# Attention steps of a hybrid diffusion layer: a finished tile's bank counts as free one step later, and two readouts are queued behind the maximum of their own step

## The chip, the core and the metric

The program runs on one core of a Trainium2 chip. The time is the device time of one execution in microseconds (us). The kernel before took 1681.66 us, the median of three runs (1681.48, 1681.66, 1682.79).

## What is computed

Two layers of a backbone work on 512 latent tokens with a prefix of 256 context tokens. The change lies in layer 0, whose mixer has two groups of heads that share one input projection and one output projection: four heads of gated linear attention (GLA, two pairs) and eight heads of softmax attention.

```python
def _gated_readout(o, og, gain):
    return _merge(_rms(o, gain) * jax.nn.silu(og))

def _softmax_attend(q, k, v):
    s = jnp.einsum('bhgqd,bhkd->bhgqk', q, k, preferred_element_type=jnp.float32) * (ATT_HEAD_DIM ** -0.5)
    p = jax.nn.softmax(s, axis=-1).astype(v.dtype)
    return jnp.einsum('bhgqk,bhkd->bhgqd', p, v)

    a_lat = _gated_readout(dirs[0][1] + dirs[1][1], og[:, :, n_ctx:], gla_out_norm)
    ...
    o_lat = jnp.concatenate([a_lat, b_lat], axis=-1)
```

A latent query sees all 768 keys, a context query the 256 context keys. The readout of the GLA heads is a root mean square over the 128 columns of a head, times a gate; its gain comes in later.

## The kernel before

**Order of the work.** `even_mixer` writes TensorE's order by hand: generators, one letter each, are advanced by `run("...")`, and every matmul and transpose that they issue is kept in that order. What VectorE (DVE), ScalarE (ACT), GpSimd (POOL) and the DMA queues do is traced in the same order, but a scheduler decides where each instruction then stands in its engine's queue; it may put an instruction forward to where its inputs are expected ready. A queue is worked off in its order. `issue_after(ins)` keeps the instructions of a block behind `ins` on the engine of `ins`; on other engines it does nothing. `net.mark` is the latest such `ins` that some helper left.

**A step of the attention over latent tokens** (`Attention.latent`, letter "y"). There are four tiles of 128 queries (t = 0 to 3) and eight heads, so step i, from 0 to 36, has head i % 8 of tile i // 8:

- `scores` multiplies the head's queries with all keys into a tile S (two buffers of two PSUM banks each), DVE takes the maximum of each row (`amx`, line 193; the keys carry a minus sign, so it is written as a minimum), ACT takes the exponential and its sum (line 195), DVE inverts the sum (`ars`, line 196) and scales the row (`prob`, line 198).
- `turned` transposes the probabilities of the head three steps earlier (j = i - 3) on TensorE: four blocks of 128 keys into a bank with the tag "tr", then two blocks into one of two banks "sc0" and "sc1". ACT copies each part out to `probT` (line 210); for every fourth head (j % 4 = 3) DVE copies the second part.
- `values`, in every other step, multiplies the probabilities of two heads with the values. It adds into the tile `attO`, which for query tile t is the whole bank "sc" t % 2 for eight steps.
- After a tile's fourth pair (step 11, 19, 27, 35) `done` reads that bank twice: ACT writes the rounded half (line 734), and DVE subtracts it from the bank for the rest (line 735).

`other()` picks the bank for the two last blocks of `turned`. As long as tile t is not in `ended` it is the bank that tile t does not use; once t is in `ended`, it is tile t's own bank, since the next tile is about to take the other one. `done` enters the tile in `ended`, so the next step's transposes (step 12, 20, 28) already go to the bank that `done` is reading. The first `values` of tile t + 1 come in step 13, 21, 29.

The 256 context queries come first, in wider steps (`Attention.context`, letter "x"), through the same helpers.

**The readouts.** `readout(c, (t0,))` treats two tiles of tokens of the pair of heads c: ACT squares (line 1188), DVE sums (`ss`, line 1190), DVE scales and adds (`ms`, line 666), POOL raises to the power -1/2 (`rs`, line 668), DVE multiplies (`gvo<-gvo,rs`, line 1193) and multiplies with the gate (`gvo<-gvo,og`, line 1195). For the second pair, c = 1, the letter is "r1"; its three parts (context tokens, latent tiles 0 and 1, latent tiles 2 and 3) are advanced behind steps 7, 10 and 15:

```python
            behind = {6: "t", 7: "r1", 9: "t", 10: "r1", 14: "M", 15: "r1", 16: "M", 17: "t", 19: "t", 22: "t", 24: "t", 26: "t", 29: "t"}
            for i in range(3, 32 + 5):
                run("y " + behind.get(i, ""))
```

The transposes "t" (`catT`, lines 1290 and 1291) read what the readouts write: the second pair's from step 22 on. "M" is a product for the modulation of the next part (`mod_acc`), which in step 14 has 64 matmuls.

Of the kernel before, what the change touches and what calls it, by code (L numbers as in the profile page):

```python
# [13 lines left out]
ALU = mybir.AluOpType  # L14
AX = mybir.AxisListType
# [118 lines left out]
class Attention:  # L134
# [43 lines left out]
    def scores(self, t, heads, p):  # L178

        nc, net = self.nc, self.net  # L180
        s = net.mm_tile("S")
        nk = p.shape[-1]
        w = 1024 // len(heads)
        for x, hd in enumerate(heads):
            at = w * x
            for ks in self.k[int(t >= LT)]:
                m = ks[0].shape[-1]
                for i, k in enumerate(ks):
                    net.mm(s[:, at : at + m], self.q[t][:, hd, :], k[:, hd // 4, :], start=(i == 0), stop=(i == 1))
                at += m  # L190
        sv = s.rearrange("p (x k) -> p x k", k=w)[:, :, :nk]
        mx, sm, r = (net.sm.tile([P, len(heads)], F32, tag=tag, name=tag) for tag in (("amx", "asm", "ars") if len(heads) == 1 else ("ms4", "ss4", "rs4")))
        nc.vector.tensor_reduce(mx, sv, axis=AX.X, op=ALU.min)
        for x in range(len(heads)):
            nc.scalar.activation(p[:, x, :], sv[:, x, :], AF.Exp, bias=mx[:, x : x + 1], scale=-1.0, accum_out=sm[:, x : x + 1])
        nc.vector.reciprocal(r, sm)
        for x in range(len(heads)):
            nc.vector.tensor_scalar(p[:, x, :], p[:, x, :], r[:, x : x + 1], None, op0=ALU.mult)
# [30 lines left out]
                )  # L229

    def done(self, t):
        self.ended.append(t)
        self.net.put(self.cat, slice(4, 8), slice(t * P, (t + 1) * P), self.po[t].rearrange("p (j i) -> p j i", j=4))

    def context(self):
# [38 lines left out]
        values(1)  # L274
        yield
        self.done(LT)
        turned(2)
        yield
        values(2)
# [1 line left out]
        yield  # L281
        values(3)
        self.done(LT + 1)

    def latent(self, ap):
        kl = [ap.tile([P, 2, SEQ], F32R, name=f"k{x}") for x in "HL"]
# [5 lines left out]
        yield  # L292

        ahead = 3
        ps, pTs, due = {}, {}, []
        for i in range(8 * LT + ahead + 2):
            t, hd = divmod(i, 8)
            if t < LT:
                ps[i] = ap.tile([P, NT], F32, tag="prob", bufs=4, name="prob")
                self.scores(t, (hd,), ps[i][:, None, :])  # L300
            j = i - ahead
            if 0 <= j < 8 * LT:
                pTs[j] = ap.tile([P, NTT, P], F32, tag="probT", bufs=4, name="probT")
                self.turned(ps.pop(j), pTs[j], (1,) if j % 4 == 3 else (), self.other())
            if due:
                t0, n, xs = due.pop()
                self.values(t0, n, xs)
                if n == 3:
                    self.done(t0)
            if 0 <= j < 8 * LT and j % 2:  # L310
                due.append((j // 8, j // 2 % 4, [pTs.pop(x) for x in (j - 1, j)]))
            if t + 1 < LT and hd == 4:
                self.queries(t + 1, q(t + 1))
            yield


class Net:
# [761 lines left out]
    def even_mixer(self, h, mix, z):  # L1079
# [102 lines left out]
        def readout(c, tiles=tiles):  # L1182
# [12 lines left out]
                nc.vector.scalar_tensor_tensor(x, x, 0.5 if c else 1.0, og[c][:, t0 : t0 + 2, :], op0=ALU.mult, op1=ALU.mult)  # L1195


        kinds = {
            "q": lambda: nat(1536 + 288, ev_q), "kv": lambda: nat(1536 + 544, ev_kv), "m": lambda: mods,
            "qk0": lambda: qk(0), "qk1": lambda: qk(1), "v0": lambda: values(0), "v1": lambda: values(1),  # L1200
            "g0": lambda: gates(0), "g1": lambda: gates(1), "p": lambda: self.att_prep(mixg, natq, natk),
            "c0": lambda: job(0, 0), "l0": lambda: job(0, 1), "c1": lambda: job(1, 0), "l1": lambda: job(1, 1),
            "e": decays, "r0": lambda: (readout(0, (t,)) for t in tiles), "r1": lambda: (readout(1, (t,)) for t in tiles),
            "x": lambda: att.context(), "y": lambda: att.latent(ap),
            "t": lambda: self.gated_T(lambda t, hh: gv[:, t, hh * P : (hh + 1) * P], 4, R_GG, cat, ((4, 2), (0, 4))),
            "M": lambda: self.mod_group(0, 4, ["wL"] * 4 + ["wH"] * 3 + ["raw"]),
# [999 lines left out]
```

## Time and profile before

| | |
|---|---|
| median of the runs | 1681.66 us |
| time of the profiled execution | 1680.08 us |
| its span in the trace | 1678.3 us |
| mean granted TensorE clock | 0.999 |
| TensorE busy | 1638.8 us, 98% of the span |
| DVE, ACT, POOL busy | 1312.2 us, 916.9 us, 122.6 us |
| attention over latent tokens | from about 256 us to 348 us of the span |

A row of the timeline has the start in us from the span's start, the time it took, engine, line, operation, output and inputs, their size and the number of instructions; in brackets stands the time that the engine was idle just before, and who ended it. Rows of one engine overlap a little, since an engine begins an instruction before the last one has fully ended. So what an instruction costs its queue is the distance to the next start, which is less than the duration by some 0.08 us on DVE and ACT.

### The profile page before, as it was taken

The page shows a single profiled execution, that of the slowest core. Times are in us where ns is not written, and L with a number is a line of the kernel's source. Part 1 is how long each engine was busy: PE and PEld are TensorE (multiplying, and loading weights), DVE is VectorE, ACT ScalarE, POOL GpSimd, SP SyncE. Part 2 cuts the span into 40 slices and gives each one's busy share as a digit, 9 for nine tenths or more (in the row PEclk, how much of TensorE's full clock was granted, in tenths as well). Part 3 has the DMA queues.
Part 4 walks back from the last instruction along what each step waited for, and adds up shares of the span by engine and source line. Part 5 has one row for each costly group of instructions (what it writes and reads, how often), then busy time and mean ns, then how long its engine had stood idle before and what let it go on. Part 6 is the DMA issues. An engine that isn't in the chain of part 4 may idle for free.

```text
span 1678.3 us, 32400 instructions
## 1 busy us (share of the span) xinstructions
PE 1638.8 (98%) x13347; PEld 1474.3 (88%) x13347; DVE 1312.2 (78%) x2104; ACT 916.9 (55%) x1560; POOL 122.6 (7%) x129
## 2 busy tenths in 40 slices
PE   6999998999999999999999999999999999999998
PEld 5889987888999999998887788888888899999886
DVE  4889768966898989778668648788775499987887
ACT  4745557846544443445447536566564565555564
POOL 1004210001000000002101000000000100000310
PEclk9999999999999999999999999999999999999999
DMA  9651002154253446249516542111115334433973
GB/s 331 193 155 41 2 28 101 52 198 152 90 151 101 134 148 193 78 136 222 101 56 210 193 132 64 52 54 50 52 56 159 117 113 122 115 101 101 223 166 138
DMA packets 184736, 204.77 MB, mean 122 GB/s; under 512 B 7143, under 2 KB 141837, under 8 KB 184589
## 3 DMA queue, kind: packets, MB, share of 16 engines
q1 hardware_dynamic: 173632, 181.82, 34.6%
q0 software_dynamic: 9024, 17.30, 5.9%
q10 hardware_dynamic: 1932, 3.59, 0.6%
q8 instruction: 104, 1.70, 0.4%
q14 instruction: 44, 0.35, 0.1%
HBM read 193.23 MB, written 9.46 MB: 121 GB/s over the span
## 4 chain that ended last, share of the span: by engine, by line
PE 84%; DVE 7%; ACT 4%; DMA 2%; issue 2%; POOL 1%; DVEq 0%; ACTq 0%; POOLq 0%
PE nat L355 12%; PE a L355 11%; PE ff L355 8%; PE E L355 8%; PE x L355 6%; PE oproj L355 6%; PE o L355 4%; PE b L355 4%; PE D L355 4%; PE pearly L355 3%; PE fq L355 3%; PE gqk L355 2%; PE q L355 2%; PE S L355 2%; PE poh L355 1%
## 5 line engine op out<-in xcount | busy, mean ns | idle before, releaser
L355 PE MATMUL nat<-wH,x 128*128 128x256 f32 (+2 forms) x968 | 226.1, 322 | 3.1 <-ACT x L734 2.6
L355 PEld LDWEIGHTS nat<-wH,x 128*128 128x128 f32 x968 | 162.0, 190 | 20.5 <-ACT x L734 4.2
L824 ACT CAST wH<-raw 128x1024 fp32r<-128x1024 f32 x120 | 124.9, 1051 | 99.0 <-DVE raw L849 37.6
L825 DVE TENSOR_TENSOR wL<-raw,wH 128x1024 fp32r<-128x1024 f32 x120 | 145.7, 1221 | 23.2 <-ACT wH L824 22.6
L355 PE MATMUL nat<-wL,x 128*128 128x256 f32 (+2 forms) x484 | 153.5, 317 | 1.8 <-DVE wL L770 1.8
L770 DVE TENSOR_TENSOR wL<-raw,wH 128x1024 fp32r<-128x1024 f32 (+1 forms) x83 | 98.7, 1198 | 49.7 <-ACT wH L769 49.0
L355 PE MATMUL ff<-x,wH 128*128 128x512 f32 (+1 forms) x512 | 127.7, 340 | 0.0
L769 ACT CAST wH<-raw 128x1024 fp32r<-128x1024 f32 (+1 forms) x83 | 84.9, 1035 | 70.6 <-PE ff L355 19.9
L668 POOL TENSOR_TENSOR rs<-ms,neghalf 128x1 f32<-128x1 f32 (+2 forms) x62 | 64.7, 1049 | 791.1 <-DVE ms L666 791.0
L355 PE MATMUL oproj<-wH,x 128*128 128x512 f32 x320 | 102.3, 396 | 0.6 <-ACT x L1290 0.6
L355 PEld LDWEIGHTS nat<-wL,x 128*128 128x128 f32 x484 | 92.1, 190 | 7.9 <-DVE wL L770 2.7
L355 PEld LDWEIGHTS ff<-x,wH 128*128 128x128 f32 x512 | 87.2, 190 | 10.0
L597 DVE SCALAR_TENSOR_TENSOR macc<-mraw,scT,macc 128x1024 f32<-128x1024 f32 x70 | 88.0, 1280 | 8.8 <-DMA mraw<-in_mod_w_dram 8.4
L355 PE MATMUL x<-wH,two 128*128 128x512 f32 x280 | 90.6, 392 | 0.8 <-DVE y L1801 0.7
L976 ACT COPY qkh<-arr 128x512 f32<-128x512 f32 x112 | 70.1, 642 | 36.4 <-DVE arr L981 32.2
L1723 POOL DMA_DIRECT2D t<-in_ffn_w_down_dram x36 | 41.8, 1198 | 637.2 <-DVE t L1762 337.5
L355 PE MATMUL ff<-x,wL 128*128 128x256 f32 (+1 forms) x256 | 86.2, 337 | 0.0
L849 DVE TENSOR_TENSOR raw<-raw 128x512 f32<-128x512 f32 x120 | 82.8, 690 | 2.8
L981 DVE TENSOR_TENSOR arr<-arr,f 128x512 f32<-128x512 f32 x112 | 74.2, 687 | 1.9 <-ACT qkh L976 0.3
L355 PEld LDWEIGHTS oproj<-wH,x 128*128 128x128 f32 x320 | 59.5, 188 | 12.8 <-ACT x L1290 1.1
L355 PE MATMUL E<-x,wH 128*128 128x384 f32 (+1 forms) x320 | 70.7, 310 | 0.0
L355 PE MATMUL b<-x,wH 128*128 128x384 f32 (+1 forms) x320 | 70.6, 310 | 0.0
(420 smaller groups left out, 4530.2 us busy)
## 6 DMA issues: line engine op xcount, KB each, us to landing
mraw<-in_mod_w_dram SPq DMA_DIRECT2D x80, 512.0 KB, 4.1
raw<-in_ffn_w_gate_dram SPq DMA_DIRECT2D x44, 512.0 KB, 4.8
raw<-in_ffn_w_up_dram SPq DMA_DIRECT2D x44, 512.0 KB, 4.4
raw<-in_odd_w_in_dram SPq DMA_DIRECT2D x40, 512.0 KB, 3.7
t<-in_ffn_w_down_dram POOLq DMA_DIRECT2D x30, 512.0 KB, 8.7
raw<-in_ffn_w_down_dram SPq DMA_DIRECT2D x28, 512.0 KB, 7.9
mraw<-in_mod_w_dram SPq DMA_DIRECT2D x32, 256.0 KB, 6.3
raw<-in_even_w_in_dram SPq DMA_DIRECT2D x16, 512.0 KB, 6.8
```

The costliest lines, as they stand in the source:

```text
L355: return self.pin(self.nc.tensor.matmul(*a, **k))
L597: nc.vector.scalar_tensor_tensor(a, u, w, a, op0=ALU.mult, op1=ALU.add)
L668: nc.gpsimd.tensor_tensor(rs, ms, self.neghalf.to_broadcast([P, w]), op=ALU.pow)
L769: nc.scalar.copy(H[:, :m], raw[:, :m])
L770: nc.vector.tensor_tensor(L[:, :m], raw[:, :m], H[:, :m].bitcast(F32), op=ALU.subtract)
L824: self.nc.scalar.copy(H, f)
L825: self.nc.vector.tensor_tensor(L, f, H.bitcast(F32), op=ALU.subtract)
L849: add = lambda o, x, y: nc.vector.tensor_tensor(o, x, y, op=ALU.add)
L976: nc.scalar.copy(qkv[:, :, :, half, :], dst)
L981: nc.vector.tensor_tensor(dst, dst, tb, op=ALU.mult)
L1723: add = lambda o, src: self.pin(nc.gpsimd.dma_start(out=o, in_=src, accum_op=ALU.add))
```

## The change

Two things. First, `done` no longer enters its tile in `ended`. In `latent` it is entered one step later, after that step's transposes have picked their bank; in `context` it is entered right behind `done`, as it was. Second, the parts of "r1" are traced with their DVE instructions kept behind the maximum (`amx`) of the step in which they are advanced, for which `scores` leaves that instruction in `net.mark`.

```diff
-        nc.vector.tensor_reduce(mx, sv, axis=AX.X, op=ALU.min)
+        net.mark = nc.vector.tensor_reduce(mx, sv, axis=AX.X, op=ALU.min)
...
     def done(self, t):
-        self.ended.append(t)
         self.net.put(self.cat, slice(4, 8), slice(t * P, (t + 1) * P), self.po[t].rearrange("p (j i) -> p j i", j=4))
...
         self.done(LT)
+        self.ended.append(LT)
...
         self.done(LT + 1)
+        self.ended.append(LT + 1)
...
-        ps, pTs, due = {}, {}, []
+        ps, pTs, due, past = {}, {}, [], []
...
+            now = []
             if due:
                 t0, n, xs = due.pop()
                 self.values(t0, n, xs)
                 if n == 3:
                     self.done(t0)
+                    now.append(t0)
+            self.ended += past
+            past = now
...
+        def later():
+            for t in tiles:
+                with self.tc.issue_after(self.mark.ins):
+                    readout(1, (t,))
+                yield
...
-            "e": decays, "r0": lambda: (readout(0, (t,)) for t in tiles), "r1": lambda: (readout(1, (t,)) for t in tiles),
+            "e": decays, "r0": lambda: (readout(0, (t,)) for t in tiles), "r1": later,
```

The change adds eleven lines, so the same statement has a higher line number after it: 735 becomes 740, 1190 becomes 1195, 1193 becomes 1198, 1195 becomes 1200; lines up to 231 keep theirs.

On DVE, at the passage from the context queries to the latent ones, two of the three readouts stood before like this (`kL` and `qs` are keys and queries for the latent steps, `x_3656` is `done` of the first context tile, `probT_3659` the copy of transposed probabilities of the context's third block):

```order
L210 COPY probT_3551<-pT 128x512 [waits PE_49]
L1190 TENSOR_REDUCE ss_3922<-sq 128x4
L1190 TENSOR_REDUCE ss_4023<-sq 128x4 [waits Activation_49]
L666 TENSOR_SCALAR ms<-ss_3922 128x4 [waits DVE_49]
...
L162 SCALAR_TENSOR_TENSOR kL<-kT,kH 64x512 [waits Activation_49]
L175 TENSOR_TENSOR qs_3592<-qT,qs_3592 64x512 [waits Activation_49]
L1193 TENSOR_TENSOR gvo<-gvo,rs 128x2x256 [waits Pool_49]
L1195 SCALAR_TENSOR_TENSOR gvo<-gvo,og_656 128x2x256 [waits DVE_49]
L735 TENSOR_TENSOR x_3656<-attO,x_3655 128x4x128 [waits PE_49,Activation_49]
L1178 SCALAR_TENSOR_TENSOR og_656<-og_656,nat 128x512 [waits Activation_49]
L210 COPY probT_3659<-pT 128x512 [waits PE_49]
```

After the change the same place on DVE has no readout:

```order
L210 COPY probT_3551<-pT 128x512 [waits PE_49]
L196 RECIPROCAL rs_3540<-ss_3539 128x4 [waits Activation_49]
...
L162 SCALAR_TENSOR_TENSOR kL<-kT,kH 64x512 [waits Activation_49]
L175 TENSOR_TENSOR qs_3592<-qT,qs_3592 64x512 [waits Activation_49]
L740 TENSOR_TENSOR x_3656<-attO,x_3655 128x4x128 [waits PE_49,Activation_49]
L1183 SCALAR_TENSOR_TENSOR og_656<-og_656,nat 128x512 [waits Activation_49]
L210 COPY probT_3659<-pT 128x512 [waits PE_49]
```

Four instructions of each of the two readouts have left this place, and so have their two on POOL; the squares on ACT have not moved. The third readout, behind step 15, stands between the same DVE instructions as before.

The second of the two moved readouts (`ss_4023`) now stands on DVE in steps 10 to 12, from the DVE copy of step 10 to `done` of query tile 0 (`x_3656`), which had only `amx`, `ars` and `prob` ahead of it:

```order
L210 COPY probT<-pT 128x256 [waits PE_49]
L1195 TENSOR_REDUCE ss_4023<-sq 128x4
L193 TENSOR_REDUCE amx<-S 128x1 [waits PE_49]
L196 RECIPROCAL ars<-asm 128x1 [waits Activation_49]
L671 TENSOR_SCALAR ms<-ss_4023 128x4 [waits DVE_49]
L198 TENSOR_SCALAR prob<-prob,ars 128x768 [waits DVE_49]
L1198 TENSOR_TENSOR gvo<-gvo,rs 128x2x256 [waits Pool_49]
L196 RECIPROCAL ars<-asm 128x1 [waits Activation_49]
L193 TENSOR_REDUCE amx<-S 128x1 [waits PE_49]
L1200 SCALAR_TENSOR_TENSOR gvo<-gvo,og_656 128x2x256 [waits DVE_49]
L198 TENSOR_SCALAR prob<-prob,ars 128x768 [waits DVE_49]
L740 TENSOR_TENSOR x_3656<-attO,x_3655 128x4x128 [waits Activation_49]
```

The first one (`ss_3922`) stands in the same manner among the `amx`, `ars` and `prob` of steps 7 to 9, ahead of that copy. On TensorE the order of these steps is the same; what the two last blocks of steps 12 and 13 wait for is not. Before, from the scores of step 12 on (`qs_3808` are the queries of tile 1):

```order
L358 MATMUL pT<-ident,prob 128x128 x4
L358 MATMUL pT<-ident,prob 128x128 [waits DVE_49,PE_49]
L358 MATMUL pT<-ident,prob 128x128
L358 MATMUL qT<-ident,natq 128x128 [waits Activation_49]
L358 MATMUL qT<-ident,natq 128x128 x3
L355 MATMUL S<-kH,qs_3808 128x512 [waits Activation_49]
...
L358 MATMUL pT<-ident,prob 128x128 [waits Activation_49]
L358 MATMUL pT<-ident,prob 128x128 x3
L358 MATMUL pT<-ident,prob 128x128 [waits Activation_49]
```

And after:

```order
L363 MATMUL pT<-ident,prob 128x128 x4
L363 MATMUL pT<-ident,prob 128x128 [waits Activation_49]
L363 MATMUL pT<-ident,prob 128x128
L363 MATMUL qT<-ident,natq 128x128 x4
L360 MATMUL S<-kH,qs_3808 128x512 [waits Activation_49]
...
L363 MATMUL pT<-ident,prob 128x128 [waits DVE_49,Activation_49]
L363 MATMUL pT<-ident,prob 128x128 x3
L363 MATMUL pT<-ident,prob 128x128 [waits DVE_49]
```

The wait of the fifth block for DVE has passed from step 12 to step 13, and step 12 waits for an ACT copy. Steps 20 and 28 change in the same way. At the end of the stage three matmuls of the output projection, which stood together between the two parts of step 32's transposes, are now spread: one between the parts of step 31's, one in step 32, one in step 33.

## The prediction, on record before the run

> **What bounds the kernel.** I begin with the page: the busy time of the engines, and the shares of the chain that ended last.
>
> ```profile
> PE 1638.8 (98%) x13347; PEld 1474.3 (88%) x13347; DVE 1312.2 (78%) x2104; ACT 916.9 (55%) x1560; POOL 122.6 (7%) x129
> ...
> PE 84%; DVE 7%; ACT 4%; DMA 2%; issue 2%; POOL 1%; DVEq 0%; ACTq 0%; POOLq 0%
> ```
>
> TensorE (PE) is busy for 98% of the span, and the chain runs on it for 84%. A change that touches no matmul can gain only what PE waits. So the next view is the table of windows over the stage that changes (window, its length, then busy time and instructions of PE, weight loads, DVE, ACT, POOL).
>
> ```profile
> 250.00:262.00 12.00, 9.93 (x89) 8.64 (x89) 10.87 (x19) 4.31 (x8) 2.96 (x5) 1.00 0.44 139
> 270.00:280.00 10.00, 9.76 (x102) 8.25 (x97) 8.89 (x17) 8.33 (x19) 0.00 (x0) 1.00 0.01 2
> 280.00:290.00 10.00, 8.42 (x77) 7.14 (x72) 7.73 (x15) 7.55 (x17) 0.00 (x0) 1.00 0.00 0
> ```
>
> From 250 to 262 us, where two readouts stand, DVE is nearly full and PE idles for about 2 us. From 270 to 290, where the change puts them, DVE works 16.6 of 20 us: room, but not much. The waits of PE from 235 to 352 us (total, times, longest) name the idle time:
>
> ```profile
> PE pT L358 <- DVE x L735: 2.1, 3, 1.3
> PE attO L355 <- DVE probT L210: 1.4, 1, 1.4
> PE pT L358 <- DVE kL L162: 0.6, 1, 0.6
> ```
>
> All three are waits for DVE, and the change touches each.
>
> **Part one: two readouts leave the passage.** DVE and PE there, from the timeline:
>
> ```profile
> 246.98 1.27 DVE L1190 TENSOR_REDUCE ss<-sq 128x4 f32<-128x512 f32 x2
> 248.17 0.29 DVE L666 TENSOR_SCALAR ms<-ss 128x4 f32<-128x4 f32 x2
> 249.51 0.69 DVE L1193 TENSOR_TENSOR gvo<-gvo,rs 128x512 f32<-128x512 f32 x1 [0.87 <-POOL rs L668]
> 252.95 1.14 DVE L1195 SCALAR_TENSOR_TENSOR gvo<-gvo,og 128x512 f32<-128x512 f32 x1
> 254.12 0.69 DVE L162 SCALAR_TENSOR_TENSOR kL<-kT,kH 64x512 fp32r<-64x512 f32 x1
> 255.57 0.69 DVE L1193 TENSOR_TENSOR gvo<-gvo,rs 128x512 f32<-128x512 f32 x1
> 256.30 0.69 DVE L1195 SCALAR_TENSOR_TENSOR gvo<-gvo,og 128x512 f32<-128x512 f32 x1
> 257.02 0.69 DVE L735 TENSOR_TENSOR x<-attO,x 128x512 fp32r<-128x512 f32 x1
> 258.22 0.68 DVE L210 COPY probT<-pT 128x512 f32<-128x512 f32 x1
> ...
> 254.96 1.35 PE L358 MATMUL pT<-ident,prob 128*128 128x128 f32 x8 [0.61 <-DVE kL L162]
> ...
> 258.96 0.66 PE L355 MATMUL attO<-probT,natk 128*64 128x128 f32 x8 [1.36 <-DVE probT L210]
> ```
>
> PE waits 0.61 us for the second `kL`, which ended at 254.81. Ahead of it went the wait for POOL with a multiplication (0.87 us idle, then 0.69 us) and the 1.14 us gate. Without them it ends more than 2 us earlier; PE's own matmuls fill its time until 254.35, so all of the 0.61 goes.
>
> The second wait, 1.36 us, is for the copy at 258.22. The two `gvo` rows at 255.57 and 256.30 hold DVE for 257.02 - 255.57 = 1.45 us directly ahead of the three instructions that end in this copy. Without them, and behind a `kL` that is no longer late, the copy ends at about 256.9, when PE, itself 0.61 us earlier, wants it (258.96 - 1.36 - 0.61 = 257.0). I leave 0.1 us of wait. **Term one: -0.61 - 1.36 + 0.10 = -1.87 us.** With the bounds 0 (DVE finds something else to be late with) and -1.97 this is the term I trust most, since nothing else moves on DVE there. The readouts issue no DMA. Their squares stay in two buffers until `ss` has read them; the next to want one is the third readout's square in step 15, when both are free.
>
> **Part two: the first readout in steps 7 to 9.** It adds to DVE's queue `ss` (two starts 0.60 us apart, since 1.27 us for two that overlap by 0.08), `ms` (0.12) and the two `gvo` rows (0.72 each, from the starts 255.57, 256.30, 257.02): 2.16 us. What DVE had free between step 7 and the copy of step 10, at 283.11, shows in the brackets:
>
> ```profile
> 276.30 0.16 DVE L196 RECIPROCAL ars<-asm 128x1 f32<-128x1 f32 x1 [0.39 <-ACT prob L195]
> 276.79 0.96 DVE L193 TENSOR_REDUCE amx<-S 128x1 f32<-128x768 f32 x1 [0.33 <-PE S L355]
> 280.44 0.16 DVE L196 RECIPROCAL ars<-asm 128x1 f32<-128x1 f32 x1 [0.55 <-ACT prob L195]
> 281.58 0.75 DVE L1291 SCALAR_TENSOR_TENSOR x<-catT,col,x 128x512 fp32r<-128x512 f32 x1 [0.32 <-ACT x L1290]
> ```
>
> 0.39 + 0.33 + 0.55 + 0.32 = 1.59 us, and `ss`, put between an `ars` and the scaling that waits for it, fills another 0.12. What is late is then the copy of step 10, by 2.16 - 1.59 - 0.12 = 0.45 us, for which PE already waits 0.27 (the row at 283.58 below). Bounds: 0, if steps 8 and 9 have slack that no bracket shows, and 2.16, if none of the free time can be used. **Term two: +0.45.**
>
> **Part three: the bank and the second readout.** Steps 10 to 13 in the timeline:
>
> ```profile
> 283.11 0.41 DVE L210 COPY probT<-pT 128x256 f32<-128x256 f32 x1
> 283.44 0.95 DVE L193 TENSOR_REDUCE amx<-S 128x1 f32<-128x768 f32 x1
> 283.58 0.44 PE L358 MATMUL pT<-ident,prob 128*128 128x128 f32 x2 [0.27 <-DVE probT L210]
> ...
> 285.54 0.38 ACT L210 COPY probT<-pT 128x256 f32<-128x256 f32 x1
> 285.88 0.62 DVE L198 TENSOR_SCALAR prob<-prob,ars 128x768 f32<-128x768 f32 x1
> 286.22 0.60 PE L358 MATMUL pT<-ident,prob 128*128 128x128 f32 x4
> 287.29 0.68 DVE L735 TENSOR_TENSOR x<-attO,x 128x512 fp32r<-128x512 f32 x1
> 288.12 0.41 PE L358 MATMUL pT<-ident,prob 128*128 128x128 f32 x2 [1.30 <-DVE x L735]
> 288.37 0.60 PE L358 MATMUL qT<-ident,natq 128*128 128x128 f32 x4
> 288.72 0.48 PE L355 MATMUL S<-kH,qs 128*128 128x512 f32 x1
> 289.51 0.82 PE L358 MATMUL pT<-ident,prob 128*128 128x128 f32 x6
> ```
>
> Step 12 wants the bank that `done` reads, and waits 1.30 us for the subtraction at 287.29. In the other bank its last reader is the ACT copy that ends at 285.92, before PE's 286.8: this wait goes. The wait that takes its place is in step 13, whose last blocks need the finished bank. PE would be there at 286.8 + 0.25 (two transposes, 288.12 to 288.37) + 0.35 (`qT`) + 0.79 (`S`) + 0.43 (four blocks) = 288.6 us. With DVE's old order the bank is free at 287.97 and step 13 finds it so.
>
> But the second readout now stands ahead of the subtraction. From the copy's start at 283.11: 0.33 to the next start, `ss` 0.60, `amx` 0.87, `ars` 0.08, which puts `ms` at 284.99. From `ms` to the multiplication there is a round through POOL; before, it took from 248.17 to 249.51, 1.34 us, and only one scaling fills it. Then `gvo` 0.72, `ars` 0.07, `amx` 0.87, `gvo` 0.72, `prob` 0.54 (285.88 to 286.42), the subtraction 0.68: 284.99 + 1.34 + 3.60 = 289.9, and PE restarts some 0.15 later, as it did at 288.12 after 287.97. That is 290.1 against 288.6: a new wait of about 1.5 us in place of 1.30. Bounds: 0, if POOL answers in the time of the scaling and DVE starts without a backlog; 2.8, if the 0.6 us round through POOL falls in twice and nothing overlaps. I take the sum. **Term three: -1.30 + 1.50 = +0.20.** The 64 matmuls of step 14 then cover DVE's backlog; without that cover it would go on into steps 15 and 16.
>
> Steps 20 and 28 have no readout. Step 20 never waited (the 2.1 us above are three waits, and the first, 0.29 us, is for a context tile, whose order in `ended` stays). Step 28 waited here:
>
> ```profile
> 331.51 0.44 PE L358 MATMUL pT<-ident,prob 128*128 128x128 f32 x2 [0.49 <-DVE x L735]
> ```
>
> Step 29 is some 1.4 us behind it and the subtraction is over by then. **Term four: -0.49**, with 0 as its other end if the matmul of the output projection that now stands in step 31 waits for its weights instead.
>
> **The sum** against the profiled execution is -1.87 + 0.45 + 0.20 - 0.49 = -1.71, so 1680.08 - 1.71 = 1678.4 us. The median of the runs is 1.58 us above that execution; the same change gives **1680.0 us**, 0.10% faster. What measurements of this kernel can tell from no change is about 0.2%, 3.4 us.
>
> **The rivals.**
>
> *All waits go.* DVE fits both readouts in, and terms two and three become 0 and -1.30: -1.97 - 1.30 - 0.49 = -3.76, 1677.9 us. For it speaks that DVE had 3.4 free us from 270 to 290; against it, that the second readout stands directly ahead of the subtraction. 0.25.
>
> *DVE becomes the bound of steps 7 to 13* and the kernel is slower. Its rows there wait for ACT's exponentials, so perhaps none of the free time is free at the right moment. Then the readouts cost 2.16 us and 2.16 + 0.6 us (POOL) in full, 4.92, against -1.87 - 1.30 - 0.49: +1.26, 1682.9 us. The point from which it decides: the waits removed come to 3.66 us, so the change loses once less than 1.26 us of DVE's free time can be used. 0.11.
>
> *The change does not do what it says in the total.* What attention wins is lost at the next place that cannot come earlier, a load above all: 1681.7 us. Over the whole run PE's list of waits has one DMA, at the start:
>
> ```profile
> PE pt_rows L358 <- DMA rows<-in_mod_b_dram: 8.0, 1, 8.0
> ```
>
> This speaks against it. 0.08.
>
> *DVE and POOL block each other.* Two rows show what the scaling `prob` does beside POOL. The first is its group from the tile's view (minimum, median, maximum in ns); the second ran inside POOL's round of the third readout, which is the row behind it.
>
> ```profile
> L198 DVE TENSOR_SCALAR prob<-prob,rs x16: 342/348/700, 230.0 to 251.3; 128x256 f32<-128x256 f32 x16
> ...
> 301.84 0.61 DVE L198 TENSOR_SCALAR prob<-prob,ars 128x768 f32<-128x768 f32 x1
> ...
> 301.21 1.28 POOL L668 TENSOR_TENSOR rs<-ms,neghalf 128x4 f32<-128x4 f32 x1 [45.72 <-DVE ms L666]
> ```
>
> One of the 16 took 0.70 us instead of 0.35; the one beside `rs` took its usual 0.61. If the scalings in the new places were held until `rs` is done, the multiplications would start 0.54 us after POOL instead of at once, less what they lose anyway: 0.36 in the first readout and 0.51 in the second, together +0.87, 1680.9 us. [...] 0.08.
>
> **How the numbers follow.** My forecast has 0.48. The range 1677.6 to 1682.6 reaches from just below the case in which all waits go to just short of the one in which DVE is the bound, and takes in the bounds of terms two and three one at a time. Faster by over 0.2% (below 1678.3) is most of the first rival, 0.18, and 0.03 of the forecast with a larger term: 0.21. Slower by over 0.2% (above 1685.0) needs the DVE rival with more than its price: 0.05. Within 0.2%: 0.74.
>
> **What would show it.** In the profile after, the waits of 0.61 and 1.36 us at the passage are gone and PE runs through from 249 to 262 us (term one). The wait for `probT` in step 11 is about 0.7 us (term two). PE's wait for the subtraction, now line 740, is no longer in step 12 but in step 13, at some 1.5 us (term three), and it is gone in step 28 (term four). I am wrong if step 13 does not wait, if new waits for `amx` or for ACT's exponentials appear between 272 and 300 us, or if the output projection begins 1.7 us earlier and the end does not.

## The result and the profile after

The changed kernel took 1679.54 us, the median of 20 runs (1678.13 to 1680.67), against 1681.74 us for the kernel before, the median of 20 runs (1680.07 to 1683.45). The ratio is 0.9987 with a 95% interval of 0.9981 to 0.9993: 2.20 us, 0.13%, faster. The forecast was 1680.0 us, 0.10%.

The two profiled executions do not show that: 1680.08 us before, 1680.65 us after. The first lies 1.66 us below the median of its kernel, the second 1.11 us above the median of its own. A part of that stands outside the stage that changed: the first row below starts 0.72 us later after the change, and another 1.1 us go between 1370 and 1412 us of the span. So the stage has to be read by itself, from one matmul ahead of the passage to one at its end. Three rows of TensorE's timeline serve for it: the transposes `kT` ahead of the passage, the 64 matmuls of step 14, and the last matmuls of `attO`. Before the change (the fourth row is step 13):

```profile
246.34 0.66 PE L358 MATMUL kT<-ident,natk 128*128 128x128 f32 x4 [0.27 <-ACT probT L210]
290.26 1.53 PE L355 MATMUL attO<-probT,natk 128*64 128x128 f32 x24
293.26 3.66 PE L355 MATMUL mod_acc<-mraw,scT 128*32 128x256 f32 x64
345.44 1.52 PE L355 MATMUL attO<-probT,natk 128*64 128x128 f32 x22
```

After it:

```profile
247.06 0.66 PE L363 MATMUL kT<-ident,natk 128*128 128x128 f32 x4 [0.27 <-ACT probT L210]
289.27 1.53 PE L360 MATMUL attO<-probT,natk 128*64 128x128 f32 x24
292.29 3.66 PE L360 MATMUL mod_acc<-mraw,scT 128*32 128x256 f32 x64
343.85 1.52 PE L360 MATMUL attO<-probT,natk 128*64 128x128 f32 x22
```

From the first row to the last it is 345.44 - 246.34 = 99.10 us before and 343.85 - 247.06 = 96.79 us after: **the stage is 2.31 us shorter**, as the median is 2.20 us lower. Of this 46.92 - 45.23 = 1.69 us fall ahead of step 14 (the front part) and 52.18 - 51.56 = 0.62 us behind it (the back part). Two more profiles of the changed kernel gave 96.79 and 96.77 us, so this length repeats within some 0.02 us, where the 20 whole runs lie up to 2.54 us apart.

The windows of after, in the same stretches as before (length, then busy time and instructions of PE, weight loads, DVE, ACT, POOL):

```profile
250.00:262.00 12.00, 11.62 (x103) 10.21 (x101) 8.62 (x16) 5.33 (x12) 2.12 (x4) 1.00 0.52 166
270.00:280.00 10.00, 9.76 (x96) 8.28 (x95) 9.52 (x20) 8.22 (x19) 1.27 (x1) 1.00 0.01 2
280.00:290.00 10.00, 8.08 (x79) 6.81 (x79) 9.04 (x18) 7.34 (x17) 1.37 (x1) 1.00 0.00 0
```

At the passage PE now works 11.62 of 12 us where it had worked 9.93, and DVE's 10.87 us have become 8.62. In 270 to 290 DVE is busy for 18.56 of 20 us instead of 16.62. PE's waits from 235 to 352 us after the change (total, times, longest):

```profile
PE pT L363 <- DVE x L740: 1.7, 2, 1.4
PE pT L363 <- DVE probT L210: 0.5, 1, 0.5
...
PE oproj L360 <- ACT prob L195: 0.5, 1, 0.5
...
PE attO L360 <- DVE probT L210: 0.3, 1, 0.3
```

The wait for `kL` (0.6) is gone, that of `attO` for `probT` (1.4) has shrunk to 0.3, the three waits for the subtraction to two, and a wait for `oproj` is new. Where they stand, in the timeline of after, on PE, DVE and POOL (the row at 254.79 is the last matmul ahead of the passage's transposes):

```profile
252.30 0.69 DVE L162 SCALAR_TENSOR_TENSOR kL<-kT,kH 64x512 fp32r<-64x512 f32 x1
254.79 0.28 PE L360 MATMUL nat<-wH,x 128*128 128x256 f32 x1
254.91 1.04 PE L363 MATMUL pT<-ident,prob 128*128 128x128 f32 x8
255.61 0.69 DVE L740 TENSOR_TENSOR x<-attO,x 128x512 fp32r<-128x512 f32 x1 [1.89 <-ACT x L739]
256.81 0.69 DVE L210 COPY probT<-pT 128x512 f32<-128x512 f32 x1
257.55 0.66 PE L360 MATMUL attO<-probT,natk 128*64 128x128 f32 x8 [0.28 <-DVE probT L210]
...
282.47 0.44 PE L363 MATMUL pT<-ident,prob 128*128 128x128 f32 x2 [0.53 <-DVE probT L210]
...
283.86 0.15 DVE L671 TENSOR_SCALAR ms<-ss 128x4 f32<-128x4 f32 x1
283.98 0.62 DVE L198 TENSOR_SCALAR prob<-prob,ars 128x768 f32<-128x768 f32 x1
284.09 1.37 POOL L673 TENSOR_TENSOR rs<-ms,neghalf 128x4 f32<-128x4 f32 x1 [7.18 <-DVE ms L671]
285.12 0.82 PE L363 MATMUL pT<-ident,prob 128*128 128x128 f32 x6
285.49 0.69 DVE L1198 TENSOR_TENSOR gvo<-gvo,rs 128x512 f32<-128x512 f32 x1 [0.90 <-POOL rs L673]
285.77 0.60 PE L363 MATMUL qT<-ident,natq 128*128 128x128 f32 x4
286.91 0.60 PE L363 MATMUL pT<-ident,prob 128*128 128x128 f32 x4
287.03 0.68 DVE L1200 SCALAR_TENSOR_TENSOR gvo<-gvo,og 128x512 f32<-128x512 f32 x1
288.16 0.68 DVE L740 TENSOR_TENSOR x<-attO,x 128x512 fp32r<-128x512 f32 x1
288.90 0.44 PE L363 MATMUL pT<-ident,prob 128*128 128x128 f32 x2 [1.39 <-DVE x L740]
...
329.44 0.82 PE L363 MATMUL pT<-ident,prob 128*128 128x128 f32 x6
336.66 0.50 PE L360 MATMUL oproj<-wH,x 128*128 128x512 f32 x1 [0.47 <-ACT prob L195]
```

Before, the last matmul and the transposes stood further apart (the transposes are the row at 254.96 in the prediction):

```profile
254.07 0.28 PE L355 MATMUL nat<-wH,x 128*128 128x256 f32 x1
```

At the passage the second `kL` is over at 252.99, two us before PE's transposes at 254.91, and DVE even stands idle for 1.89 us. Step 11 waits 0.53 us where it had waited 0.27. Step 12's transposes at 285.12 run through. Step 13, at 288.90, waits 1.39 us for the subtraction of 288.16, which stands behind the readout's two multiplications and the 0.90 us that DVE waits for POOL. Step 28, at 329.44, no longer waits.

### The profile page after: what moved, and what is told of

It is laid out like the page before. It is cut to its first block, busy times and chain, and to the rows that moved or that the text cites. A ratio compares the mean times of both kernels' runs of the same rounds, so it can differ in the third digit from the quotient of the medians.

```text
span 1678.5 us, 32403 instructions
## 1 busy us (share of the span) xinstructions
PE 1640.1 (98%) x13347; PEld 1475.6 (88%) x13347; DVE 1310.7 (78%) x2104; ACT 916.6 (55%) x1560; POOL 125.8 (7%) x129
## 4 chain that ended last, share of the span: by engine, by line
PE 79%; DVE 10%; ACT 5%; DMA 3%; issue 2%; POOL 1%; SPq 0%; DVEq 0%; ACTq 0%; POOLq 0%
PE nat L360 12%; PE a L360 10%; PE ff L360 8%; PE E L360 7%; PE x L360 6%; PE oproj L360 6%; PE o L360 4%; PE b L360 3%; PE D L360 3%; PE fq L360 3%; PE gqk L360 2%; PE pearly L360 2%; PE q L360 2%; PE poh L360 1%; PE S L360 1%
## 5 line engine op out<-in xcount | busy, mean ns | idle before, releaser
L360 PE MATMUL E<-T,wH 128*128 128x384 f32 (+1 forms) x320 | 70.4, 309 | 0.4 <-DVE go L907 0.4
L360 PE MATMUL a<-T,wH 128*128 128x384 f32 (+1 forms) x320 | 70.4, 309 | 0.3 <-ACT qb L892 0.3
```

Source lines behind the costliest of these rows:

```text
L360: return self.pin(self.nc.tensor.matmul(*a, **k))
```

## The experiments

**The theory** is the prediction's: which wait PE has is set by where the readouts stand in DVE's queue, ahead of the copy at the passage or ahead of `done`'s subtraction, and by which bank the last blocks go to. **The rival** is that DVE is simply full, and hands a wait on by a step, whatever stands where. Each kernel is the changed one with one edit. The table takes the three rows shown above (`kT`, the 64 matmuls, the last `attO`) from each profile; the times of the runs stand beside them. The kernel before was timed again beside most of them, with medians of 1681.64 to 1681.86 us where it had 19 or more runs.

| kernel | front part | back part | stage | against before | us (runs) |
|---|---|---|---|---|---|
| before | 46.92 | 52.18 | 99.10 | | 1681.74 (20) |
| changed | 45.23 | 51.56 | 96.79 | -2.31 | 1679.54 (20) |
| bank alone | 45.77 | 51.54 | 97.31 | -1.79 | 1680.33 (1) |
| readouts alone, first profile | 48.69 | 52.18 | 100.87 | +1.77 | 1683.58 (1) |
| readouts alone, second profile | 47.07 | 52.22 | 99.29 | +0.19 | 1682.14 (10) |
| second readout behind step 13 | 43.80 | 52.65 | 96.45 | -2.65 | 1681.16 (1) |
| readouts behind 6 and 12 | 43.78 | 51.98 | 95.76 | -3.34 | 1678.74 (11) |
| second readout cut around the subtraction | 43.77 | 51.76 | 95.53 | -3.57 | 1676.86 (1) |
| the same, timed | 43.78 | 51.75 | 95.53 | -3.57 | 1677.22 (9) |
| second readout not kept behind | 44.63 | 51.51 | 96.14 | -2.96 | 1677.81 (1) |
| second readout cut, sum a step earlier | 44.82 | 51.57 | 96.39 | -2.71 | 1677.74 (1) |
| first readout at the passage | 45.14 | 51.59 | 96.73 | -2.37 | 1678.39 (1) |

**The changed kernel again.** No edit; for what two profiles of one kernel differ by.

> The changed kernel once more, for what two profiles of one kernel differ by. All theories expect the same waits as in its first profile, within 0.05 us each: 1.39 us in step 13, 0.53 us in step 11, none at the passage above 0.3 us. The start of the first matmul and the late feed-forward blocks may differ by some 0.7 to 1.2 us, as they did between the first profiles of the two kernels.

Measured: the same list of waits, a stage of 96.79 us, and `kT` at 246.77 in place of 247.06. The stage repeats; what lies ahead of it does not.

**The bank alone.**

```diff
-            ... "r1": later,
+            ... "r1": lambda: (readout(1, (t,)) for t in tiles),
```

> Only the bank changes: a tile is entered one step later, the three readouts are traced as in the kernel before. My theory (the terms are set by where the readouts stand in DVE's queue): the two waits of the passage stay, 0.61 and 1.36 us. Step 12 no longer waits for the subtraction (1.30 us before) and step 13 does not wait for it either, less than 0.2 us, since nothing stands ahead of it; step 28's 0.49 us goes. In sum the attention over latent tokens ends 1.6 to 2.0 us earlier than in the kernel before, all of it behind 288 us of the span. Rival (the wait only moves on by a step, whatever stands on DVE): step 13 waits 1.0 to 1.5 us for the subtraction, and the stage ends 0.4 to 0.8 us earlier.

Measured: -1.79 us, and the list of waits has the 1.4 and 0.6 of the passage again. Step 12 and step 13 do not wait. DVE's rows in the timeline show why: nothing but `ars`, `prob` and `amx` stands between the copy and the subtraction, which is over at 288.24.

```profile
286.68 0.96 DVE L193 TENSOR_REDUCE amx<-S 128x1 f32<-128x768 f32 x1
287.56 0.68 DVE L740 TENSOR_TENSOR x<-attO,x 128x512 fp32r<-128x512 f32 x1
```

The rival falls here: a bank handed over one step later does not bring a wait of its own.

**The readouts alone.**

```diff
                 if n == 3:
                     self.done(t0)
-                    now.append(t0)
-            self.ended += past
-            past = now
+                    self.ended.append(t0)
```

> Only the readouts change their place; the finished bank counts as free at once, as in the kernel before. My theory: the passage gains the same as in the changed kernel, 2.0 to 2.2 us. Step 11 waits about 0.5 us for the copy of step 10. Step 12 wants the bank that the subtraction reads, and the subtraction stands behind the second readout: a wait of 2.8 to 3.3 us in place of 1.30. Step 28 keeps its 0.49 us. In sum the stage ends between 0.6 us earlier and 0.4 us later than in the kernel before: the two edits need each other. Rival (two independent edits, whose gains add up to the 2.3 us of the changed kernel): step 12 keeps 1.30 us, and the stage ends 1.6 to 2.0 us earlier.

Measured: step 12 waits 3.28 us, as expected, so the rival (two independent edits) falls; but the stage is 1.77 us longer, outside what any theory said. The difference is not in the waits. Windows of this profile, with the granted clock in the last column but two:

```profile
290.00:291.00 1.00, 1.00 (x8) 0.96 (x7) 0.55 (x1) 0.42 (x1) 0.00 (x0) 0.65 0.00 0
291.00:292.00 1.00, 1.00 (x6) 0.67 (x7) 0.97 (x2) 0.49 (x1) 0.00 (x0) 0.50 0.06 16
292.00:293.00 1.00, 1.00 (x12) 1.00 (x12) 0.39 (x2) 0.95 (x4) 0.00 (x0) 0.50 0.00 0
293.00:294.00 1.00, 1.00 (x16) 0.98 (x12) 0.42 (x1) 0.99 (x3) 0.00 (x0) 0.65 0.00 0
```

PE is busy all the time, but its clock goes from 1.00 to 0.50, for (1.00 - 0.65) / 0.50 = 0.70 us of the first of these windows, two whole ones, and 0.70 of the last: 3.4 us. The 24 matmuls of `attO` in step 13 take 2.45 us in this profile instead of 1.53:

```profile
288.95 0.41 PE L360 MATMUL pT<-ident,prob 128*128 128x128 f32 x2 [3.28 <-DVE ars L196]
...
291.77 2.45 PE L357 MATMUL attO<-probT,natk 128*64 128x128 f32 x24
```

(The wait is put down to `ars`, whose record is the last on DVE ahead of it; the subtraction stands directly before that, from 288.12 to 288.81.) Whether such a wait always costs the clock was tried by the same kernel once more.

> The readouts alone once more. In its first profile PE waited 3.28 us in step 12, and then the granted clock stood at 0.50 from about 290.4 to 293.8 us, in which the same matmuls took twice as long: 1.6 us on top of the wait. Theory (a wait of that length is answered by half the clock, whatever the run): the same drop at the same place, the stage 1.7 to 1.9 us later than in the kernel before, and a median 1.5 to 2.2 us above it. Rival (the drop was a chance of one execution, as the drop to half at 106 us in the profile of the kernel with the second readout behind step 13 was, where the same wait of 1.8 us left the clock alone in five other profiles): no drop at 290 us, the stage 0.0 to 0.3 us later, a median within 0.5 us of the kernel before.

Measured: the wait is 3.27 us, and the clock stays at 1.00. The stage is 0.19 us longer than before, the median of ten runs 1682.14 us, and the ratio 1.0003 with an interval of 0.9994 to 1.0012. So the expectation for the edit holds where the clock holds, and the drop belongs to one execution, not to the program. The passage gains its 2.13 us here too (`kT` at 245.91, the transposes behind `attO` at 256.99, against 246.34 and 259.55 before), and step 12 gives it back. The bank alone gives -1.79, the readouts alone +0.19, together -2.31 and not -1.60: the readouts pay only with the bank, and then 0.52 us; the bank pays without them.

```profile
287.83 0.41 PE L360 MATMUL pT<-ident,prob 128*128 128x128 f32 x2 [3.27 <-DVE ars L196]
```

**The second readout behind step 13.**

```diff
-            behind = {..., 7: "r1", 9: "t", 10: "r1", 14: "M", 15: "r1", ...}
+            behind = {..., 7: "r1", 9: "t", 13: "r1", 14: "M", 15: "r1", ...}
```

> The changed kernel with its second readout advanced behind step 13 in place of step 10. My theory: step 13's wait for the subtraction (1.39 us) goes, below 0.2 us, because the readout stood ahead of the subtraction; at 290 us the same matmul starts 2.3 to 2.6 us earlier than in the kernel before, against 0.98 us in the changed kernel. The readout then lies directly ahead of the third one, and DVE's backlog of steps 14 to 16 may give back 0.5 to 1.4 us behind the 64 matmuls of step 14: at the end of the stage between 1.7 and 3.6 us earlier than before. Rival (the wait of step 13 belongs to the hand-over of the bank, not to the readout): step 13 keeps over 1 us and the stage ends 2.3 us earlier, as in the changed kernel.

Measured: step 13 does not wait, so the rival (the wait belongs to the hand-over of the bank) falls, and the front part is 3.12 us shorter than before. (The figure of 2.3 to 2.6 for 290 us was made with the 0.72 us by which the profile of after is late ahead of the passage left in; without them it is 3.0 to 3.3.) The back part is 1.09 us longer than in the changed kernel: DVE now has the second and third readout one behind the other. Behind step 14 PE waits 0.79 us for a buffer of scores that ACT's exponential has yet to read, 0.42 in the changed kernel (the exponential itself waits 0.59 us for `amx` on DVE), and 0.46 us for an ACT copy of `probT`, for which the changed kernel does not wait.

The stage wins 0.34 us over the changed kernel, and yet this run took 1681.16 us: its profile lost about 1.7 us (half of 3.4) to the clock far from here; the last section shows it.

**Readouts behind steps 6 and 12.**

```diff
-            behind = {6: "t", 7: "r1", 9: "t", 10: "r1", ...}
+            behind = {6: "t r1", 9: "t", 12: "r1", ...}
```

> The changed kernel with its first readout behind step 6 (in place of 7) and its second behind step 12 (in place of 10). My theory (the wait goes wherever no readout stands between the maximum and the subtraction): the passage gains 2.1 us as in the changed kernel; step 11 waits 0.3 to 0.6 us; no wait over 0.2 us in step 13, so that at 290 us the same matmul starts 3.1 to 3.4 us earlier than in the kernel before (the offset at 236 us taken off); in steps 14 to 16, behind the 64 matmuls, 0.4 to 0.9 us of it goes to DVE's backlog; at 345 us 2.8 to 3.3 us earlier, against 2.3 in the changed kernel. The median of the runs then lies 0.5 to 1.0 us below the changed kernel's. Rival (DVE is the bound of steps 10 to 16 and only hands the wait on): at 345 us 2.3 us earlier, plus or minus 0.2.

Measured: -3.34 us, at the upper end of what was expected, so the rival's 2.3 falls. No wait in step 13; step 11 still waits 0.54 us; behind step 14 PE waits 0.83 us for a buffer of scores. The median is 1678.74 us, against 1681.86 for the kernel before beside it, and the ratio 0.9981 (0.9972 to 0.9990).

**The second readout cut in two around the subtraction**: sum, `ms` and `rs` behind step 10, the two multiplications behind step 12.

```diff
-            behind = {..., 10: "r1", 14: "M", ...}
+            behind = {..., 10: "r1", 12: "r1", 14: "M", ...}
...
+                    with self.tc.issue_after(self.mark.ins):
+                        rs = readout(1, (t,), True)
+                    yield
+                    with self.tc.issue_after(self.mark.ins):
...
+                        nc.vector.tensor_tensor(o, o, rb, op=ALU.mult)
+                        nc.vector.scalar_tensor_tensor(x, x, 0.5, og[1][:, t : t + 2, :], op0=ALU.mult, op1=ALU.mult)
```

> The changed kernel with the second readout cut in two: sum, scaling and POOL's power behind step 10 as before, the two multiplications behind the maximum of step 12, so behind the subtraction. It takes the 0.90 us for which DVE waited for POOL, and the two multiplications, out of the stretch ahead of the subtraction, and leaves the sum there. My theory: step 13's wait of 1.39 us is this 0.90 plus two multiplications of 0.69, and goes to below 0.2 us; at 290 us 3.1 to 3.4 us earlier than in the kernel before (the offset at 236 us taken off), at 345 us 2.8 to 3.3 us. Rival (the sum of 0.68 us and the maxima alone keep DVE late): step 13 still waits 0.5 us or more.

Measured: -3.57 us, more than expected. On DVE the subtraction now stands ahead of both multiplications:

```profile
285.86 0.69 DVE L740 TENSOR_TENSOR x<-attO,x 128x512 fp32r<-128x512 f32 x1
286.46 0.68 DVE L1215 TENSOR_TENSOR gvo<-gvo,rs 128x512 f32<-128x512 f32 x1
...
288.50 0.68 DVE L1216 SCALAR_TENSOR_TENSOR gvo<-gvo,og 128x512 f32<-128x512 f32 x1
```

Counted from `kT`, the subtraction starts at 285.86 - 246.22 = 39.64 us against 288.16 - 247.06 = 41.10 in the changed kernel: 1.46 us earlier, enough for the 1.39. The sum alone does not keep DVE late. This is the best version, so it was timed, beside the changed kernel on the same chip.

> The second readout cut in two around the subtraction, once more and timed. My theory: the stage ends 3.5 to 3.6 us earlier than in the kernel before, as in its first profile, 1.2 to 1.3 us earlier than in the changed kernel, and the median of the runs lies 2.9 to 4.2 us below the kernel before and 0.6 to 1.9 us below the changed kernel of the same chip. Rival (what the stage gains is lost again later): the median is within 0.5 us of the changed kernel's.

> The changed kernel, timed on the same chip beside the version with the second readout cut in two. All theories: 1.5 to 3.0 us below the kernel before, the same waits as in its first two profiles, 1.39 us in step 13.

Measured: 1677.22 us (median of 9) against 1678.96 us (11) for the changed kernel and 1681.64 us (19) for the kernel before. The ratios to the kernel before are 0.9976 (0.9966 to 0.9986) and 0.9984 (0.9975 to 0.9993). The 1.74 us between the two medians are in the range that was expected; the 4.42 us to the kernel before are a little beyond theirs. The version beats both.

**The sum a step earlier, the multiplications where they were.** This separates POOL's round from the multiplications.

```diff
-            behind = {..., 7: "r1", 9: "t", 10: "r1", ...}
+            behind = {..., 7: "r1", 9: "t r1", 10: "r1", ...}
```

(the readout cut as above)

> The changed kernel with the second readout cut in two otherwise: sum, scaling and POOL's power one step earlier, behind step 9, and the two multiplications behind step 10, where they were. So the 0.90 us for which DVE waited for POOL's answer is gone from the stretch ahead of the subtraction, but the two multiplications of 0.69 us stay in it. My theory (the wait of step 13 is POOL's round plus what stands ahead): step 13 waits 1.39 - 0.90 = 0.4 to 0.6 us; the sum now stands ahead of the copy of step 10, so step 11 waits 0.8 to 1.1 us in place of 0.53; at 345 us 2.3 to 2.8 us earlier than in the kernel before (offset at 236 us taken off). Rival (POOL's round is hidden beside other waits of DVE): step 13 keeps 1.2 us or more.

Measured: step 11 waits 0.95 us, as expected; step 13 does not wait at all, where 0.4 to 0.6 us were expected; and the 64 matmuls of step 14 wait 0.58 us until DVE is through with `qs`.

```profile
281.59 0.44 PE L363 MATMUL pT<-ident,prob 128*128 128x128 f32 x2 [0.95 <-DVE probT L210]
285.84 0.68 DVE L740 TENSOR_TENSOR x<-attO,x 128x512 fp32r<-128x512 f32 x1
290.61 3.66 PE L360 MATMUL mod_acc<-mraw,scT 128*32 128x256 f32 x64 [0.58 <-DVE qs L175]
```

Counted from `kT` (245.79), the subtraction starts at 40.05, 1.05 us earlier than in the changed kernel; and PE, held up in step 11, comes 0.95 - 0.53 = 0.42 us later. 1.39 - 1.05 - 0.42 is below zero. The expectation had left out that PE itself is late. That the 0.58 us of step 14 are what remains of DVE's backlog is likely, but no run separates it.

**The second readout not kept behind anything**, the first and third as in the changed kernel.

```diff
+                if t == tiles[1]:
+                    readout(1, (t,))
+                else:
                     with self.tc.issue_after(self.mark.ins):
                         readout(1, (t,))
```

> Only the first and the third readout are kept behind the maximum of their step; the second is traced behind step 10 without that, and so stands on DVE at the passage, as in the kernel before. My theory: the passage had two readouts too many by one; its second wait (1.36 us) was the multiplications of both and the first (0.61 us) the wait for POOL ahead of them, so that one readout alone leaves a wait of 0.1 to 0.8 us and the passage gains 1.3 to 2.1 us of the 2.13. Step 13's wait for the subtraction falls from 1.39 to below 0.3 us, since nothing stands ahead of the subtraction in steps 10 to 12; at 345 us 2.2 to 3.4 us earlier than in the kernel before. Rival (each readout costs the passage the same half): the passage gains 1.0 to 1.1 us.

Measured: -2.96 us, but the expectation took for granted that the second readout would go back to the passage. It did not: the scheduler put it directly behind the first with its sum ahead of the copy of step 10.

```profile
278.05 0.67 DVE L1195 TENSOR_REDUCE ss<-sq 128x4 f32<-128x512 f32 x1
...
282.89 0.69 DVE L1198 TENSOR_TENSOR gvo<-gvo,rs 128x512 f32<-128x512 f32 x1 [0.19 <-POOL rs L673]
```

So this run says nothing on the passage. On step 13 it agrees with the last experiment: with POOL's answer nearly there (0.19 us in place of 0.90) the wait for the subtraction is gone, and step 11 waits 0.89 us.

**The first readout at the passage**, the second and third as in the changed kernel (`tiles[0]` in the edit above).

> The second and the third readout are kept behind the maximum of their step, the first is traced as in the kernel before: so one readout stands on DVE at the passage, ahead of the second kL, and one in steps 10 to 12. Theory (the passage has room for one readout: what made PE wait was the two multiplications of the second one ahead of the copy, and the gate beside POOL's cast ahead of kL): the passage still gains 1.5 to 2.1 us of 2.13; step 11 waits 0.27 us as in the kernel before, since steps 7 to 9 hold no readout; step 13 keeps 1.3 to 1.4 us. At 345 us 2.0 to 2.6 us earlier than in the kernel before. Rival (each readout costs the passage half): the passage gains 1.0 to 1.1 us, and the stage ends 1.4 to 1.6 us earlier.

Measured: -2.37 us, 0.06 more than the changed kernel.

```profile
253.93 1.35 PE L363 MATMUL pT<-ident,prob 128*128 128x128 f32 x8 [0.15 <-DVE kL L162]
281.09 0.44 PE L363 MATMUL pT<-ident,prob 128*128 128x128 f32 x2 [0.27 <-DVE probT L210]
287.52 0.44 PE L363 MATMUL pT<-ident,prob 128*128 128x128 f32 x2 [1.41 <-DVE x L740]
```

With one readout the passage keeps 1.90 of its 2.13 us: it has a wait of 0.15 us, its eight transposes take 1.35 us as before the change, and the wait of 0.28 us for the copy is gone. Step 11 is back at its 0.27. So moving the first readout is worth nothing, and the rival (half the gain for each) falls.

## Why the prediction was right, point by point

The time came 0.5 us under the forecast, inside its range, and each term of the sum was there with its sign. The sizes:

| term | predicted | measured | from rows |
|---|---|---|---|
| one: the passage | -1.87 | -2.13 | `kT` +0.72 (246.34 to 247.06); `attO` behind the copy -1.41 (258.96 to 257.55) |
| two: step 11 | +0.45 | +0.30 | -1.41 to -1.11 (283.58 to 282.47) |
| three: steps 12 and 13 | +0.20 | +0.12 | -1.11 to -0.99 (290.26 to 289.27) |
| four: step 28 and the end | -0.49 | -0.62 | the back part, 52.18 to 51.56 |
| sum | -1.71 | -2.31 | 99.10 to 96.79 (the terms, rounded, -2.33) |

All four differences, 0.08 to 0.26 us, go the same way: the gains were put too low and the prices too high. That the time still came within 0.5 us is no luck of errors that cancel. And with 20 runs of each kernel 0.13% could be told from no change, where the prediction had reckoned with 0.2%.

- **Term one** has its mechanism, and the bound of -1.97 was wrong: here the waits cost more than their brackets. The gap ahead of the eight transposes was 254.96 - 254.07 = 0.89 us before and is 254.91 - 254.79 = 0.12 now: 0.77 us for a bracket of 0.61. The transposes themselves took 1.35 us and take 1.04: a second, shorter stop among them, which no bracket shows, went with the first (in the trace of before the fifth starts 0.37 us behind the fourth, where the others are 0.11 to 0.14 apart; after the change all are 0.11 apart). The wait for the copy went from 1.36 to 0.28, 1.08 us. Together 0.77 + 0.31 + 1.08 = 2.16, as good as the 2.13 of the table, where the brackets alone give 1.69. A bracket counts from the end of the last matmul's row (254.07 + 0.28 = 254.35 for the 0.61), and in these rows the next one starts before that end when it has nothing to wait for. In the row at 285.12 six transposes and the next instruction are 0.65 us apart, so four take 0.43, but a row of four is 0.60 us long. For step 12 before, 288.12 - 286.22 - 0.43 = 1.47 us were lost where the bracket said 1.30; step 28 shortened by 0.71 us for a bracket of 0.49. I used the 0.43 to find when PE would arrive in step 13, and not to price the waits that go.
- **Term two**: the copy of step 10 held PE for 0.53 us, not 0.7. By the rows it came 0.30 us late, so DVE took in 1.86 of the readout's 2.16 us where its brackets had promised 1.71.
- **Term three** held almost to the digit: step 12's wait is gone, and step 13 waits 1.39 us (1.5 predicted) for the subtraction behind the second readout. By the rows the one cost 1.47 and the other costs 288.90 - 286.91 - 0.43 = 1.56. That the readout is the cause was shown: without it there (the bank alone, the readout behind 12 or 13, or cut) the wait is gone. POOL's 0.90 us are part of it: with POOL asked earlier the subtraction is 1.05 us earlier.
- **Term four**: step 28's wait is gone; the other end that I had named, the matmul of the output projection in step 31, waits 0.47 us, and costs 0.10 on balance.
- **All waits go** did not happen here, but it names what could be had: -3.76 us, against -3.57 measured with the second readout cut.
- **DVE becomes the bound**: DVE is busy for 18.56 of 20 us and does set the two waits that are left, but not more. Where two readouts follow each other, with the second behind step 13, the back part shows what a full DVE costs: 1.09 us.
- **The total gives it back**: 2.31 us in the stage, 2.20 in the medians. It does not.
- **DVE and POOL block each other**: not as the rival feared, yet not for nothing. The scalings lose nothing, also not the one beside `rs` (283.98 beside 284.09, 0.62 us). The group of all 32, minimum, median and maximum in ns, has no slow one:

```profile
L198 DVE TENSOR_SCALAR prob<-prob,ars x32: 609/618/623, 260.8 to 339.4; 128x768 f32<-128x768 f32 x32
```

It is POOL that loses. The same power without a scaling beside it, in the kernel with the second readout not kept behind:

```profile
281.85 1.01 POOL L673 TENSOR_TENSOR rs<-ms,neghalf 128x4 f32<-128x4 f32 x1 [5.98 <-DVE ms L671]
```

With one beside it, it takes 1.37 us at 284.09, and it took 1.28 at 301.21 before, in a row of which the prediction had read only what the scaling beside it did. So some 0.36 us of the 0.90 for which DVE waits on POOL come from DVE's own scaling (an estimate, from these two durations). Which of the two begins first makes little difference in these rows: at 284.09 the scaling had begun 0.11 us earlier and took 0.62, at 301.21 the power began 0.63 us ahead of the scaling, which took its usual 0.61. At the passage of before it was DVE that lost: the gate at 252.95 ran beside POOL's cast of `kH` (252.94, 0.61 us) and took 1.14 us, where the other one, at 256.30, took 0.69.

Two things the prediction did not see: the version with the first readout left alone would have done as well, and most of what the second costs in step 13 (1.26 of 1.56 us) could be avoided by where it is cut.

## What to carry to other kernels

A wait that one edit removes can be held by the queue of another engine: ask what stands ahead of the instruction that frees the buffer, since here the later bank alone won 1.79 us, the moved readouts alone nothing (+0.19), both together 2.31, and the order around the subtraction another 1.26. Cut a helper that goes through a second engine and back at that round, and let the urgent instruction pass between its halves. And where whole runs scatter by more than an edit is worth, measure from one matmul to another around it.

## What the runs showed of the hardware

**Twice a wait was followed by half of TensorE's clock, and mostly it was not.** The step 12 of the readouts alone waited 3.28 us and was followed by 3.4 us at a granted clock of 0.50 in one profile, and 3.27 us at 1.00 in the other; the difference in the stage was 100.87 - 99.29 = 1.58 us. A second case stands far ahead of the change, at 104 us, where PE waits in every kernel for a copy on DVE. In the profile with the second readout behind step 13:

```profile
105.64 0.86 PE L363 MATMUL modT<-ident,modrows 128*128 128x128 f32 x4 [1.82 <-DVE modrows L474]
```

```profile
106.00:108.00 2.00, 2.00 (x11) 2.00 (x10) 2.00 (x4) 0.00 (x0) 0.00 (x0) 0.50 0.90 309
108.00:110.00 2.00, 2.00 (x13) 2.00 (x13) 2.00 (x4) 0.00 (x0) 0.00 (x0) 0.66 0.09 35
```

In the thirteen other profiles the same wait was 1.66 to 1.87 us, and the clock stayed at 1.00. Here 3.4 us again ran at half speed, behind a wait of 1.82 us where it had been 3.28 in the first case, and `kT` came at 248.65, 1.6 to 2.9 us later than in any other profile. The 1.39 us of step 13 were not followed by it in any of the three profiles of the changed kernel. In 13 of the 14 profiles, all but that with the first readout at the passage, the windows of 20 to 300 us up to 1500 us of the span show no third drop: 1.00 in each but the two that hold these, at 0.91. That the wait is the cause is likely, since both drops began within 1.4 us of its end, but it is not shown, and how often a wait of a given length is answered so cannot be said from these counts.

**What stays open** is the time between 1370 and 1412 us: against the profile of before it lost 1.1 us in the first profile of after (the same matmuls start 1.46 us earlier than before ahead of it, 0.34 us earlier behind it), though the order of PE's, DVE's and ACT's instructions there is the same. From the last `attO` row to the end of the span it is 1332.9 us before and 1334.7, 1333.9 and 1333.7 us in the three profiles of after. The two profiles of the readouts alone, one and the same program, differ there by 1.4 us (1333.9 and 1332.5), so at least a part of it is scatter between executions. Its cause was not tried.
